# A gated DeltaNet layer reordered: decays from running sums, half of z's product between the quarters of q and k, later heads between output chunks

## The chip, the cores and the metric

The kernel runs on one core of a Trainium2 chip. The metric is the device time of one execution in microseconds (us), from the start of the program to its end. Work inside a core is shared by five engines, each with its own in-order queue: TensorE (PE in the profile; PEld is its weight load), VectorE (DVE), ScalarE (ACT), GpSimd (POOL) and SyncE (SP). Transfers between the chip's memory (DRAM) and the on-chip memory (SBUF) are issued from the SP, ACT and POOL queues and run on 16 DMA engines. Matmul results land in PSUM, which VectorE and ScalarE read.

## What is computed

The reference is a decoder trunk of two layers on 256 tokens with 2048 features, in float32. Layer 0 mixes tokens with an mLSTM, layer 1 with a gated DeltaNet; each layer then attends to 256 memory tokens and applies a squared-ReLU MLP with 8192 hidden features. Each sub-layer is wrapped in two RMS norms. The change concerns the DeltaNet, cut here to what matters (16 heads of q and k, 32 heads of v, 128 features each, chunks of 64 tokens):

```python
p = h @ w_in
qkv, z, bt, a = jnp.split(p, GDN_SPLITS, axis=-1)
qkv = jax.nn.silu(causal_dwconv(qkv, conv_w))
q = l2_norm(q) * (GD_K ** -0.5);  k = l2_norm(k)
beta = jax.nn.sigmoid(bt)
g = -jnp.exp(a_log) * jax.nn.softplus(a + dt_bias)
gam = jnp.cumsum(to_chunks(g), axis=-1)
diff = gam[..., :, None] - gam[..., None, :]
A   = einsum(kb, kc) * exp(where(strict, diff, -inf))     # unit triangular systems
U   = triangular_solve(A, vb);  W = triangular_solve(A, kb * exp(gam))
Aqk = einsum(qc, kc) * exp(where(causal, diff, -inf))
# recurrence over chunks gives o, then
o = rms_norm(o, norm_g) * jax.nn.silu(z)
return o @ w_out
```

The decay between two tokens is the exponential of a difference of running sums of g.

## The kernel before

**Products.** Every weight matrix is streamed once from DRAM in units of 1 MB (class `Weights`, lines 35 to 109). The order of units is a list written out at the start (`plan`, lines 127 to 153), and every product takes the next unit from it. A unit comes in two halves of 512 KB on SP's queue; each half is split into a high part (ScalarE, L88) and a low part (VectorE, L89), so that two or three fp32r matmuls stand for one of full precision. Two units are in flight. The splits are issued under `high_priority(offset=400)` (L100), which ranks them 400 instructions earlier than their place in the code; the Tile framework orders each engine's queue ahead of time by rank, among the instructions that it expects to be ready. Three forms of product exist: `prod_feat` (L316, L317) with features on partitions, `prod_tall` (L335 to L337), which makes one block of 128 features from a unit of 2048 x 128 weights with 48 matmuls of 256 columns, and `prod_tok` (L380 to L382) with tokens on partitions, 24 matmuls of 512 columns a unit and 96 for a chunk of 512 output columns.

**The DeltaNet layer**, `gdn` (from L860), has these stages:

1. *Quarters of q and k* (loop at L1017). Quarter c makes four heads of q (`prod_q`) and of k (`prod_k`), each feature block with its convolution (`conv`, L873: a product into a padded tile on VectorE, a scaling on ScalarE, three multiply-adds on VectorE at L883, SiLU on ScalarE). After the first k come the gates g and beta (`gates`, L916).
2. *Norms and pairs.* `norms(c)` takes the L2 norms of the quarter (squares at L975, sums by matmul at L979). `pairs(grp)` serves a group of four v heads (two k heads): `decays(grp)` makes the exponentials, two matmuls a k head (L996, L997) make the products of keys and queries, VectorE applies norms and causal masks (L999, L1001) and multiplies with the decays (L1007) into a tile `at`, of which there is one buffer; it is stored to DRAM on GpSimd's queue (L1009, L1014). In the kernel before, the norms and the first group of quarter c-1 come behind q of quarter c, and the second group behind k of quarter c; the last two groups come inside v's product.
3. *decays* (L937). GpSimd multiplies a triangular mask with g's high and low parts (L946, four products of 128 x 512 a group), TensorE sums them with six matmuls of 512 columns a group (L950) into PSUM slots named gep, and ScalarE takes twelve exponentials of 128 x 128 from them (L954).
4. *v and the solver* (L1080). Eight chunks of v, stored to DRAM token by token (`store_v`), with the triangular systems solved on VectorE between them (`solve`, L1042: the load of its inputs `work` and `rki` on GpSimd's queue at L1058 and L1046, a first product at L1061, then 31 steps).
5. *Heads and output* (L1218). For each half of the heads: four times a chunk of z (`prod_tok("gz")`, with SiLU on ScalarE into `zs`) followed by the group's `core` (L1099: loads, block inverses, products with v, norm, gate, transposes, split into y), then four chunks of the output product `g_out` over that half. The result of the first half is kept in SBUF and the second half is added.

**Buffers.** PSUM has three slots for short products (`psum`) and five for accumulators (`acc`). The pool `acts` has one buffer a tag: `h0` to `h15` hold the layer's input h, `u0` to `u15` and `y0` to `y3` are reused by stage.

## Time and profile before

| | us |
|---|---|
| median of three runs | 2935.88 |
| the three runs | 2935.88, 2927.8, 2936.1 |
| the profiled execution | 2926.02 |
| its span, first to last instruction | 2924.3 |

The profiler times one execution; a row of its views gives the engine, the line of the kernel, the operation, the tile written and the tiles read, the shapes, a count, and then busy time, mean duration in ns, and the idle time of that engine just before, with what ended it. Matmuls overlap one another, so what a matmul takes of PE's order is read from start to start in the timeline, not from its duration; a full f32 matmul leaves two records. By the timeline, the DeltaNet layer's own products begin at about 1244 us. The quarters of q and k run from there to about 1472, v's product from there to 1683, the heads and the output product from 1683 to about 2129. Layer 0 lies before, the second layer's attention and MLP behind.

### The profile page before, as it was taken

The numbers are of one execution on the slowest core, as the hardware profiler recorded it, in microseconds if no ns is written. First come the engines' busy times: TensorE is split into PE (matmuls) and PEld (weight loads), VectorE is DVE, ScalarE is ACT, GpSimd is POOL, SyncE is SP. The second block draws the span as 40 slices with busy tenths as digits, with TensorE's granted clock in tenths as the row PEclk, the third lists the DMA queues.
The fourth block names the chain that finished last, engine by engine and source line by source line (L and its number), as shares of the span: only waits on it lengthen the run. The fifth ranks groups of instructions, "written<-read, shape, count | busy, mean of one in ns | idle before, by whom it ended". The sixth has DMA issues, their size and how long they took to land.

```text
span 2924.3 us, 42593 instructions
## 1 busy us (share of the span) xinstructions
PE 2870.3 (98%) x16723; PEld 2479.6 (85%) x16723; DVE 1758.4 (60%) x2538; ACT 1458.4 (50%) x2221; POOL 159.7 (5%) x298
## 2 busy tenths in 40 slices
PE   8999999999999999999999999999999999999998
PEld 7888887888888888799999978888878888888887
DVE  5555656754645555588787955445576545455565
ACT  6444545644434444467775445445465444344443
POOL 0000000000000000003232131010000000000000
PEclk9999999999999999999999999999999999999999
DMA  7545564555555565666678775665545555555555
GB/s 243 186 146 172 192 202 130 187 190 193 187 189 188 192 195 185 208 157 192 187 211 231 219 263 197 207 196 180 199 142 176 192 189 187 192 187 193 192 187 166
DMA packets 375884, 557.65 MB, mean 191 GB/s; under 512 B 23409, under 2 KB 156274, under 8 KB 373378
## 3 DMA queue, kind: packets, MB, share of 16 engines
q1 hardware_dynamic: 363456, 507.12, 55.0%
q0 software_dynamic: 10656, 46.48, 4.6%
q8 instruction: 131, 2.15, 0.3%
q10 hardware_dynamic: 1570, 1.33, 0.1%
q14 instruction: 71, 0.58, 0.1%
HBM read 529.65 MB, written 25.20 MB: 190 GB/s over the span
## 4 chain that ended last, share of the span: by engine, by line
PE 44%; DVE 3%; DMA 2%; issue 1%; ACT 1%; POOL 0%; DVEq 0%; ACTq 0%; POOLq 0%
PE up L316 8%; PE down L380 4%; PE down L381 4%; PE down L382 4%; PE up L317 4%; PE g_out L381 2%; PE g_out L382 2%; PE g_out L380 2%; PE gz L380 2%; PE gz L382 2%; PE gz L381 2%; DVE lo L89 1%; PE op L1191 1%; DVE cv L883 1%; PE gv L336 1%
## 5 line engine op out<-in xcount | busy, mean ns | idle before, releaser
L89 DVE TENSOR_TENSOR lo<-raw,hi 128x1024 fp32r<-128x1024 f32 x938 | 1112.0, 1226 | 903.1 <-ACT hi L88 901.1
L88 ACT CAST hi<-raw 128x1024 fp32r<-128x1024 f32 x938 | 936.6, 1045 | 962.9 <-PE down L382 327.1
L316 PE MATMUL up<-h,hi 128*128 128x512 f32 x1920 | 678.7, 399 | 0.0
L317 PE MATMUL up<-h,lo 128*128 128x256 f32 x1920 | 539.9, 281 | 0.0
L316 PEld LDWEIGHTS up<-h,hi 128*128 128x128 f32 x1920 | 361.2, 188 | 89.2
L381 PE MATMUL down<-lo,u 128*128 128x512 f32 x1024 | 398.8, 390 | 0.0
L380 PE MATMUL down<-hi,u 128*128 128x512 f32 x1024 | 398.8, 389 | 0.0
L382 PE MATMUL down<-hi,u 128*128 128x512 f32 x1024 | 398.7, 389 | 0.0
L317 PEld LDWEIGHTS up<-h,lo 128*128 128x128 f32 x1920 | 363.3, 189 | 0.2
L382 PEld LDWEIGHTS down<-hi,u 128*128 128x128 f32 x1024 | 192.3, 188 | 40.1
L380 PEld LDWEIGHTS down<-hi,u 128*128 128x128 f32 x1024 | 192.3, 188 | 39.9
L381 PEld LDWEIGHTS down<-lo,u 128*128 128x128 f32 x1024 | 192.3, 188 | 39.5
L337 PE MATMUL gv<-h,lo 128*128 128x256 f32 x512 | 146.1, 285 | 4.8 <-DVE lo L89 4.8
L335 PE MATMUL gv<-h,hi 128*128 128x256 f32 x512 | 147.1, 287 | 0.0
L336 PE MATMUL gv<-h,hi 128*128 128x256 f32 x512 | 145.2, 284 | 0.0
L381 PE MATMUL gz<-lo,h 128*128 128x512 f32 x256 | 102.6, 401 | 1.8 <-DVE lo L89 1.8
L380 PE MATMUL gz<-hi,h 128*128 128x512 f32 x256 | 103.0, 402 | 0.1
L337 PEld LDWEIGHTS gv<-h,lo 128*128 128x128 f32 x512 | 98.2, 192 | 5.7 <-DVE lo L89 5.6
L382 PE MATMUL gz<-hi,h 128*128 128x512 f32 x256 | 102.4, 400 | 0.0
L381 PE MATMUL g_out<-lo,u 128*128 128x512 f32 x256 | 100.9, 394 | 0.5 <-DVE lo L89 0.5
L380 PE MATMUL g_out<-hi,u 128*128 128x512 f32 x256 | 100.6, 394 | 0.0
L382 PE MATMUL g_out<-hi,u 128*128 128x512 f32 x256 | 100.1, 393 | 0.0
(426 smaller groups left out, 4711.3 us busy)
## 6 DMA issues: line engine op xcount, KB each, us to landing
raw<-in_w_up SPq DMA_DIRECT2D x256, 512.0 KB, 3.9
raw<-in_w_down SPq DMA_DIRECT2D x256, 512.0 KB, 4.1
raw<-in_gdn_w_in SPq DMA_DIRECT2D x192, 512.0 KB, 4.9
raw<-in_mlstm_w_in SPq DMA_DIRECT2D x96, 512.0 KB, 4.2
raw<-in_gdn_w_out SPq DMA_DIRECT2D x64, 512.0 KB, 4.2
raw<-in_mlstm_w_out SPq DMA_DIRECT2D x32, 512.0 KB, 4.2
at_d<-at POOLq DMA_DIRECT2D x8, 1536.0 KB, 8.0
ab<-at_d POOLq DMA_DIRECT2D x8, 1536.0 KB, 6.9
```

What stands on the lines that cost most here:

```text
L88: a = nc.scalar.copy(h_, raw[:, :, :n])
L89: return a, nc.vector.tensor_tensor(l_, raw[:, :, :n], h_, ALU.subtract)
L316: PE.matmul(a[:fw], wh, srcs[kk][:, :], start=(kk == 0), stop=False, skip_group_check=True)
L317: PE.matmul(a[:fw, T:], wl, srcs[kk][:, 0:T], start=False, stop=(kk == nk - 1), skip_group_check=True)
L335: PE.matmul(a[:, 0:T], hi[k], srcs[k][:, 0:T], start=(k == 0), stop=False)
L336: PE.matmul(a[:, 0:T], hi[k], srcs[k][:, T:], start=False, stop=False)
L337: m = PE.matmul(a[:, 0:T], lo[k], srcs[k][:, 0:T], start=False, stop=(k == nk - 1))
L380: PE.matmul(accs[t], sh, hi[j], start=(kk == 0), stop=False)
L381: PE.matmul(accs[t], sh, lo[j], start=False, stop=False)
L382: PE.matmul(accs[t], sl, hi[j], start=False, stop=(kk == nk - 1))
L883: V.scalar_tensor_tensor(c, pad[:, j : j + T], w[j], c, ALU.mult, ALU.add)
L1191: PE.matmul(op[:, hh * P : (hh + 1) * P], aq[:, 1 if st else tt * 2, hh, :], w[:, st, hh * P : (hh + 1) * P], start=(hh == 0 and st == 0), ...
```

## The change

- **Decays.** The running sum of g within the 128 tokens of a tile is made once in `gates`, by two small matmuls with tokens on partitions (`cum`) and two with heads on partitions (`cumr`). `cumr` is stored to DRAM (`g_d`) and read back for each group as two tiles of 128 x 4 x 128 in which every partition holds the same rows (`load_rows`, on GpSimd's queue, two groups ahead). `decays` then forms the differences on VectorE, twelve `tensor_scalar` of 128 x 128 a group, and ScalarE takes two exponentials of 768 columns, in place. GpSimd's products, the matmuls of L950 and the split of g into two parts go.
- **Masks.** The two causal masks lie in one tile, and the eight masked products of a group become four of twice the width.
- **z.** The second half of z's product (chunks 4 to 7) moves between the quarters: quarter c makes q, k, the norms, the first group, one chunk of z (`early_z`: SiLU, store to DRAM `z_d`) and the second group. The weight plan follows. All groups are done when v's product begins.
- **Heads.** Groups 0 to 3 have their chunk of z before them as they had. Groups 4 to 7 are issued each before one of the first half's four output chunks (`later`, through the new argument `start` of `prod_tok`), with z read back from DRAM; their y is kept in the tiles of h, which is no longer needed.
- **Rank of the splits.** The offset of `high_priority` is a field `first`, 0 everywhere but in the DeltaNet layer, where it is 400 as before.

```diff
-                with self.tc.high_priority(offset=400):
+                with self.tc.high_priority(offset=self.first):
...
                 if c == 0:
                     ws.add("ab", g_in, 0, D, GDN_QKV + GDN_Z, 64, tall=True)
+                ws.add("gz", g_in, 0, D, GDN_QKV + 2048 + c * 512, 512)
             ws.add("gv", g_in, 0, D, 4096, 4096, tall=True)
+            ws.add("gz", g_in, 0, D, GDN_QKV, 2048)
             for half in range(2):
-                ws.add("gz", g_in, 0, D, GDN_QKV + half * 2048, 2048)
                 ws.add("g_out", g_out, half * 2048, 2048, 0, D)
...
+            masks = sc.tile([P, 2, P], F32, name="masks")
+            V.tensor_copy(masks[:, 0, :], tri_lt)
+            V.tensor_copy(masks[:, 1, :], tri_le)
...
                 PE.matmul(p_[:, 0:32], tri_gt, g[:, 0, :], start=True, stop=True)
+                for t in range(2):
+                    PE.matmul(p_[:, 32 + t * 32 : 64 + t * 32], tri_le, g[:, t, :], start=True, stop=True)
+                    PE.matmul(p_[0:32, P + t * P : 2 * P + t * P], g[:, t, :], tri_le, start=True, stop=True)
+                cumr = sc.tile([32, 2 * P], F32, name="cumr")
+                V.tensor_copy(cumr, p_[0:32, P : 3 * P])
+                nc.gpsimd.dma_start(g_d, cumr)
...
+            def load_rows(grp):
+                rows_of[grp] = []
+                for tt in range(2):
+                    r_ = acts.tile([P, 4, P], F32, tag=f"u{8 + grp % 2 * 2 + tt}", name="grow")
+                    src = g_d[grp * 4 : grp * 4 + 4, tt * P : (tt + 1) * P]
+                    nc.gpsimd.dma_start(r_, src.unsqueeze(0).to_broadcast([P, 4, P]))
+                    rows_of[grp].append(r_)
...
             def decays(grp):
                 dm = [acts.tile([P, 2, 3, P], F32, tag=f"y{grp % 2 * 2 + i}", name="gdm") for i in range(2)]
+                gr = rows_of.pop(grp)
+                for kh in range(2):
+                    for v2 in range(2):
+                        hh = kh * 2 + v2
                         hv = grp * 4 + hh
+                        for tt in range(2):
+                            V.tensor_scalar(dm[kh][:, v2, tt, :], gr[tt][:, hh, :], cum[:, tt, hv : hv + 1],
+                                            cml[:, tt, hv : hv + 1], ALU.min, ALU.subtract)
+                        V.tensor_scalar(dm[kh][:, v2, 2, :], gr[1][:, hh, :], sufb[:, hv : hv + 1], None, ALU.add)
+                    S.activation(dm[kh], dm[kh], AF.Exp)
+                if grp + 2 < GV_H // 4:
+                    load_rows(grp + 2)
                 return dm
...
+            def early_z(c):
+                def ev(ch, t, a):
+                    o_ = acts.tile([P, 512], F32, tag=f"u{14 + t}", name="zst")
+                    S.activation(o_, a, AF.Silu, scale=rs.tok[:, t : t + 1])
+                    nc.gpsimd.dma_start(z_d[c, :, t, :], o_)
+                prod_tok("gz", h, 1, ev)
...
             for c in range(4):
                 prod_q(c)
-                if c:
-                    norms(c - 1)
-                    pairs(c * 2 - 2)
                 prod_k(c)
                 if c == 0:
-                    lnb, gh, gl, sufb = gates()
-                else:
-                    pairs(c * 2 - 1)
+                    cum, cml, sufb = gates()
+                    load_rows(0)
+                    load_rows(1)
+                norms(c)
+                pairs(c * 2)
+                early_z(c)
+                pairs(c * 2 + 1)
             prod_v(0)
-            norms(3)
-            pairs(6)
             prod_v(1)
-            pairs(7)
             store_v(0)
...
+            y = new_u()
+            for g4 in range(4):
+                zs = gate(g4)
+                if g4 == 0:
+                    store_v(7)
+                core(g4, zs, y[g4 * 4 : g4 * 4 + 4])
+            y2 = new_h()
+
+            def later(ch):
+                zs = sc.tile([P, 2, 512], F32, tag="zs", bufs=2, name="zs")
+                nc.gpsimd.dma_start(zs, z_d[ch])
+                core(4 + ch, zs, y2[ch * 4 : ch * 4 + 4])
+
+            prod_tok("g_out", y, 4, lambda ch, t, a: post.add(ch, t, a, True), start=later)
+            prod_tok("g_out", y2, 4, lambda ch, t, a: post.take(ch, t, a, True), post=post)
...
         else:
+            ws.first = 400
             with tc.tile_pool(name="g0", bufs=1) as g0:
                 post = gdn(g0, h, xs)
+            ws.first = 0
```

More of the change, by code (lines that the diff above doesn't have):

```diff
@@ L354, in prod_few, with prod_tok @@
         return p_[:, 0 : 2 * n].rearrange("p (t n) -> p t n", t=2)
-    def prod_tok(key, srcs, n_ch, evac, after=None, post=None, stagger=False):
+    def prod_tok(key, srcs, n_ch, evac, after=None, post=None, stagger=False, start=None):
         nk = len(srcs)
         for c in range(n_ch):
+            if start:
+                start(c)
             accs = [acc(f"{key}{c}_{t}") for t in range(2)]
@@ L904, in gdn @@
         with tc.tile_pool(name="gd1", bufs=1) as sc:
-            tri_gt_r = sc.tile([P, P], F32R, name="tri_gt_r")
-            V.tensor_copy(tri_gt_r, tri_gt)
-            ones_r = sc.tile([P, P], F32R, name="ones_r")
-            V.tensor_copy(ones_r, ones)
+            masks = sc.tile([P, 2, P], F32, name="masks")
+            V.tensor_copy(masks[:, 0, :], tri_lt)
+            V.tensor_copy(masks[:, 1, :], tri_le)
             dtb = sc.tile([P, 32], F32, name="dtb")
@@ new lines, in gates @@
+                V.tensor_tensor(cml, cum, lnb, ALU.subtract)
+                return cum, cml, sufb
+            rows_of = {}
+            def load_rows(grp):
[5 more added lines that the diff above has]
+                    rows_of[grp].append(r_)
@@ L937, in decays @@
             def decays(grp):
                 dm = [acts.tile([P, 2, 3, P], F32, tag=f"y{grp % 2 * 2 + i}", name="gdm") for i in range(2)]
-                for blk, tt, lhs in ((0, 0, tri_gt_r), (1, 1, tri_gt_r), (2, 1, ones_r)):
-                    ep = psum("gep")
-                    if blk < 2:
-                        rr = []
-                        for i, src in enumerate((gh, gl)):
-                            r_ = acts.tile([P, 4, P], F32R, tag=f"u{8 + 2 * tt + i}", name=f"gl{tt}{i}")
-                            G.tensor_tensor(r_, tri_le[:, None, :].to_broadcast([P, 4, P]),
-                                            src[:, tt, grp * 4 : grp * 4 + 4].unsqueeze(2).to_broadcast([P, 4, P]), ALU.mult)
-                            rr.append(r_)
-                    for i in range(2):
-                        PE.matmul(ep, lhs, rr[i].rearrange("p h i -> p (h i)"), start=(i == 0), stop=(i == 1))
-                    for hh in range(4):
-                        hv = grp * 4 + hh
-                        b_ = sufb[:, hv : hv + 1] if blk == 2 else lnb[:, tt, hv : hv + 1]
-                        S.activation(dm[hh // 2][:, hh % 2, blk, :], ep[:, hh * P : (hh + 1) * P], AF.Exp, bias=b_)
@@ L1216, in core, with gate @@
                         split_into(ys[h2 * 2 + i], tp[:, i * T : (i + 1) * T], cols[:, COL_GDN : COL_GDN + 1])
-            for half in range(2):
-                y = new_u()
-                for g4 in range(4):
-                    zs = sc.tile([P, 2, 512], F32, tag="zs", bufs=2, name="zs")
-                    prod_tok("gz", h, 1, lambda ch, t, a: S.activation(zs[:, t, :], a, AF.Silu, scale=rs.tok[:, t : t + 1]))
-                    if half == 0 and g4 == 0:
-                        store_v(7)
-                    core(half * 4 + g4, zs, y[g4 * 4 : g4 * 4 + 4])
-                prod_tok("g_out", y, 4, (lambda ch, t, a: post.take(ch, t, a, True)) if half else
-                         (lambda ch, t, a: post.add(ch, t, a, True)), post=post if half else None)
+            def gate(g4):
+                zs = sc.tile([P, 2, 512], F32, tag="zs", bufs=2, name="zs")
+                prod_tok("gz", h, 1, lambda ch, t, a: S.activation(zs[:, t, :], a, AF.Silu, scale=rs.tok[:, t : t + 1]))
+                return zs
+            y = new_u()
[6 more added lines that the diff above has]
+            def later(ch):
+                zs = sc.tile([P, 2, 512], F32, tag="zs", bufs=2, name="zs")
+                nc.gpsimd.dma_start(zs, z_d[ch])
+                core(4 + ch, zs, y2[ch * 4 : ch * 4 + 4])
+            prod_tok("g_out", y, 4, lambda ch, t, a: post.add(ch, t, a, True), start=later)
+            prod_tok("g_out", y2, 4, lambda ch, t, a: post.take(ch, t, a, True), post=post)
         return post
```

20 lines of the change are left out of this document (10 added, 10 removed).

## The prediction

> **What bounds the kernel now.** The page comes first, then the chain, then PE's waits.
>
> ```profile
> span 2924.3 us, 42593 instructions
> PE 2870.3 (98%) x16723; PEld 2479.6 (85%) x16723; DVE 1758.4 (60%) x2538; ACT 1458.4 (50%) x2221; POOL 159.7 (5%) x298
> ```
>
> The reader is to see that TensorE (PE) is busy nearly all of the time, and no other engine is above 60% beside its weight loads. A matmul that PE needn't run shortens the kernel, as long as nothing else becomes late. 54 us are left in which PE is idle. The view of waits says who ends that idle time; I quote those that the change can touch and the largest that it leaves alone.
>
> ```profile
> PE ltp L212 <- DVE xk L492: 12.9, 8, 3.2
> PE gv L337 <- DVE lo L89: 4.8, 4, 2.5
> PE xo L380 <- ACT hi L88: 2.8, 2, 1.9
> PE g L997 <- ACT gdm L954: 2.2, 1, 2.2
> ```
>
> The first row belongs to the seams between sub-layers. The second and the fourth lie in the DeltaNet layer. The busy time by stage shows that layer: three quarters of q and k (the first three rows), then v's product while the triangular systems are solved.
>
> ```profile
> core 0: us, PE busy (x) PEld busy (x) DVE busy (x) ACT busy (x) POOL busy (x), PEclk, DMA share, GB/s
> 1322.00:1382.20 60.20, 57.73 (x442) 54.60 (x442) 48.73 (x77) 43.88 (x73) 20.03 (x31) 1.00 0.68 192
> 1382.20:1440.40 58.20, 57.95 (x446) 54.86 (x445) 47.28 (x75) 44.28 (x74) 19.42 (x34) 1.00 0.70 201
> 1440.40:1498.20 57.80, 57.80 (x447) 55.03 (x447) 46.53 (x76) 44.31 (x74) 20.29 (x34) 1.00 0.72 205
> ...
> 1557.00:1610.00 53.00, 49.19 (x407) 48.58 (x407) 39.74 (x68) 25.36 (x38) 10.34 (x23) 1.00 0.82 237
> 1610.00:1683.00 73.00, 72.02 (x602) 71.78 (x601) 68.85 (x117) 34.60 (x52) 9.13 (x20) 1.00 0.79 225
> ```
>
> In a quarter DVE is busy for 47.3 of 58.2 us (81%) and PE doesn't wait. In 1557 to 1610 PE loses 3.8 us. The clock column is 1.00 throughout, so no throttle enters the sum.
>
> **The change part by part. First, the decays.** Six matmuls a group (L950) go. I price them by what they take of PE's order, start to start, since a matmul's own duration overlaps the next.
>
> ```profile
> 1352.67 1.09 PE L950 MATMUL gep<-gl,tri_gt_r 128*128 128x512 f32 x4
> 1353.60 0.63 PE L950 MATMUL gep<-gl,ones_r 128*128 128x512 f32 x2
> 1354.07 0.28 PE L335 MATMUL gq<-h,hi 128*128 128x256 f32 x1
> ```
>
> From 1352.67 to 1354.07 are 1.40 us for the six of one group. Eight groups make 11.2 us, on the path, because PE has other work ready behind them. What comes instead on PE is four plain f32 matmuls in gates(), once: two of 32 columns and two of 128.
>
> ```profile
> 1314.80 0.30 PE L932 MATMUL suf<-g,tri_gt 128*128 128x32 f32 x2
> 1314.94 0.36 PE L337 MATMUL gq<-h,lo 128*128 128x256 f32 x1
> ```
>
> ```profile
> 1338.96 0.59 PE L997 MATMUL g<-gqk 128*128 128x256 f32 x2
> 1339.21 0.47 PE L337 MATMUL gk<-h,lo 128*128 128x256 f32 x1
> ```
>
> One of 32 columns takes 0.14 us (two records), one of 256 columns 0.25; so the four cost between 0.56 and 0.78, and I take 0.6. The net is 10.6 us off PE.
>
> The L950 products also held PSUM slots of the pool of three until ScalarE had taken the exponentials out. That is the 2.2 us row of g L997 <- gdm L954 above: the only such wait, and nothing of it remains when the exponentials read SBUF. I credit 2.2. What could be late next at this place is g's own slot, which DVE empties at L999 and L1001; it is so today in every other group without a wait of this size.
>
> The work that moves to other engines is this.
>
> ```profile
> L883 DVE SCALAR_TENSOR_TENSOR cv<-pad,cols,cv 128x256 f32<-128x256 f32 x100 | 54.4, 577 | 1.0 <-ACT gm L1003 0.2
> L999 DVE SCALAR_TENSOR_TENSOR gm<-g,rk,tri_lt 128x128 f32<-128x128 f32 x16 | 5.6, 348 | 9.0 <-PE g L996 9.0
> L954 ACT ACTIVATE gdm<-gep,lnb 128x128 f32<-128x128 f32 x64 | 18.6, 368 | 0.2
> L975 ACT ACTIVATE l2sq<-gqk 128x512 f32<-128x512 f32 x14 | 8.2, 644 | 0.0
> L88 ACT CAST hi<-raw 128x1024 fp32r<-128x1024 f32 x70 | 69.9, 1047 | 32.6 <-issue 15.3 <-PE gv L336 6.9 <-PE gq L336 3.7
> L89 DVE TENSOR_TENSOR lo<-raw,hi 128x1024 fp32r<-128x1024 f32 x69 | 88.5, 1323 | 9.7 <-ACT hi L88 9.7
> L946 POOL TENSOR_TENSOR gl<-tri_le,gl 128x512 fp32r<-128x512 f32 x16 | 21.6, 1352 | 0.0
> L946 POOL TENSOR_TENSOR gl<-tri_le,gh 128x512 fp32r<-128x512 f32 x16 | 18.0, 1122 | 33.9 <-PE gep L950 29.1 <-DVE sufb L934 4.8
> ```
>
> ```profile
> L883 DVE SCALAR_TENSOR_TENSOR cv<-pad,cols,cv x100: 393/480/4601, 1297.5 to 1545.7; 128x256 f32<-128x256 f32 x100
> ```
>
> ```profile
> L850 DVE TENSOR_SCALAR sp_r<-sp_u x1: 228/228/228, 1304.9 to 1304.9; 128x128 f32<-128x128 f32 x1
> ```
>
> ScalarE: twelve exponentials of 0.37 us a group (4.4) become two over 768 columns; between 0.64 (512 columns) and 1.05 (1024) I take 0.85 each, 1.7 in all. DVE: twelve tensor_scalar come in. The nearest row is L850 at 0.23 us, the upper bound is L999's 0.35, which reads PSUM: 2.8 to 4.2 us a group, and I take 2.8. The eight mask products of 0.35 become four of twice the width, priced by L883's median of 0.48: 2.8 becomes 1.9. GpSimd: the four products a group go. With them goes what they did to DVE: L883 has a median of 480 ns but a mean of 577 and one instruction of 4601 ns, and 97 ns times 100 are 9.7 us of DVE time over the stage, 2.4 a quarter.
>
> The Trainium skill (SBUF — State Buffer, "Who interferes with whom") states that a DVE instruction with two SBUF inputs and a GpSimd instruction that reads SBUF exclude each other for the length of the one that came first. By that rule up to all 39.6 us of the two L946 rows come off DVE, 9.9 a quarter, where L883's rows show 2.4. The trace agrees in kind (the 4601 ns). The page speaks against the change as well, under "SBUF: two separate sides": one-input DVE work in its faster mode, which tensor_scalar can be, locks out the descriptor writing of GpSimd's DMAs, and that would delay the new row loads; no run here shows it. The sum stays the same by both; they move the first rival's chance only, in opposite directions.
>
> **Second, z between the quarters.** Sixteen weight units move forward, with every DMA and split that they issue, on SP's queue in the same order as the plan. Their matmuls cost the same anywhere.
>
> ```profile
> 1909.82 0.39 PE L382 MATMUL g_out<-hi,u 128*128 128x512 f32 x1
> 1910.05 0.39 PE L380 MATMUL gz<-hi,h 128*128 128x512 f32 x1
> ```
>
> The first row is the end of one chunk and the second the start of the next, 0.23 us apart. A chunk of 96 is 22 us of PE. A quarter then has 58.2 - 2.8 + 22 = 77.4 us of PE. DVE gets 47.3 + 8 x 1.32 (z's subtractions) + 2 x (2.8 - 0.9) - 2.4 = 59.3 us, 77%, and 80% with the dearer tensor_scalar; it was 81%. ScalarE gets 44.3 + 8 x 1.05 + 2 x 0.64 - 2 x 2.7 = 48.6, 63%; it was 76%. So the extra product is paced by PE. It is also the cover that the new order needs: the squares for norms(c) now follow k's convolution at once, where q's product of the next quarter stood between (23 us); the z chunk of 22 us takes that place. Were this cover gone, one chain would stand on PE: four DVE operations near L883's 0.48 and three ScalarE operations up to 0.64, about 4 us a quarter and 16 in all. That needs PE's order to put the norms ahead of a product that is ready; with half of it I bound the new order's waits at +8, and at -2 below, and take +1.
>
> The new DMAs on GpSimd's queue (two row loads a group, two z stores a quarter) queue ahead of the stores of A and the three-column memsets that each convolution needs. Rows are asked for two groups ahead, a whole quarter of 77 us (groups 0 and 1 only when the gates are done, but no matmul waits for their decays); accumulators are five deep and a tall unit uses one, so a late memset has four units to catch up. I price both at nothing; if this cover fails, the price is the one of the next paragraph.
>
> **Third, the solver.** In the kernel before, groups 6 and 7 are still at work inside v's product, so the solver's inputs are queued late on GpSimd, and DVE runs into them:
>
> ```profile
> 1581.65 2.29 DVE L1061 TENSOR_TENSOR solve_w<-solve_w,rki 128x2048 f32<-128x2048 f32 x1 [2.28 <-DMA rki<-rk_d]
> ```
>
> ```profile
> 1584.25 2.35 DVE L89 TENSOR_TENSOR lo<-raw,hi 128x1024 fp32r<-128x1024 f32 x2
> ```
>
> ```profile
> 1585.53 0.38 PE L337 MATMUL gv<-h,lo 128*128 128x256 f32 x1 [2.47 <-DVE lo L89]
> ```
>
> DVE waits 2.28 us for the load and takes 2.29 for the product; the weights' low halves queue behind both, and PE loses 2.47. After the change all pairs end about when v's product starts, so the load lands before DVE gets there, and the twelve steps behind it don't pile up. Of the 4.8 us in the wait row I credit 3.3, between 0 and 4.8.
>
> **Fourth, later heads' cores.** Cores 4 to 7 run beside the first half's four output chunks, 4 x 22 = 88 us of PE, instead of beside z. The same matmuls interleave, and z's SiLU is read back from DRAM. I take 0, between -2 and +2.
>
> **Fifth, splits outside this layer** lose their rank of 400 instructions. That reorders ScalarE and DVE everywhere; the trace shows no such order. In the MLP there is room for it:
>
> ```profile
> 707.64 2.36 DVE L89 TENSOR_TENSOR lo<-raw,hi 128x1024 fp32r<-128x1024 f32 x2 [3.08 <-ACT hi L88]
> ```
>
> ```profile
> L401 DVE TENSOR_TENSOR j_up<-up,h_up 128x256 f32<-128x256 f32 x21 | 8.4, 419 | 0.0
> ```
>
> A unit's two subtractions take 2.36 us after 3.08 us idle. A feature's three DVE operations (0.42 each) are 1.3, which fit. Softmax chains at the seams would go ahead of splits. I take -1, between -9 (half of the 12.9 + 2.8 + 2.2 us of waits at such chains) and +63 (rival 2).
>
> The sum: -10.6 - 2.2 - 3.3 + 1 + 0 - 1 = -16.1 us. The profiled execution took 2926.0 (span 2924.3 and 1.7 around it), which gives 2910. The median of the three runs, 2935.9, lies 9.9 above it, so I forecast 2935.9 - 16 = 2920.
>
> **The rivals.** (1) The quarters are held by DVE's order, not by PE. Both groups of a quarter now crowd around the z chunk; if an instruction there waits for a late row load, or an `at` product for the stores of the group before, the low halves queue behind it as at L1061, and the 11.2 us come back as PE waits for lo. That gives 2931, no difference to be told. Against it: 77% DVE, and no such wait in 1440 to 1498. (2) The splits without rank come late in the MLP. If all four features of a chunk (4 x 1.26 = 5.0 us) go ahead of the two subtractions, 3.08 us of idle time cannot hold them, PE waits 2.0 us a chunk, and 2 layers x 16 chunks cost 63: 2983, slower. It decides once more than 3.08 us go ahead, that is three features; against it, three of the four are complete before the unit ends. (3) The seams gain their 9 us: 2911. For it, the ScalarE casts that precede softmax work; against it, much of the seams' order is fixed by hand.
>
> **How the numbers follow.** Forecast 0.65, rival one 0.14, rival two 0.09, rival three 0.12. A measurement can tell about 0.3% (8.8 us) from no change, so faster means below 2927. Forecast and rival three make 0.77 faster, less 0.02 for the forecast's upper tail: 0.75; same 0.16; slower 0.09. The range goes from 2898 (2911 less what the solver and the new order may give beyond my values, 1.5 + 3, and the 8.1 by which the fastest run lies under the median) to 2940 (2920 with +7 from the new order, +3.3 without the solver's gain, +2 for the cores and the same 8). It leaves out rival two.
>
> **What would show it.** Right: no L950; three quarters of about 77 us each with PE idle under 1 us; L883's mean near 480 ns; the wait of L1061 for rki gone, and 1557 to 1610's counterpart without its 3.8 us; PE's busy total about 11 us lower. Wrong: new PE waits for lo inside the quarters, a DVE wait for the row loads, or PE waits for hi or lo in the up products.

## The result, and the profile after

The changed kernel takes 2911.37 us (median of four executions, 2910.57 to 2916.84). The kernel before, timed beside it, takes 2932.49 (four, the three of the table above among them, 2927.8 to 2936.1). The ratio is 0.9929, with a 95% interval of 0.9916 to 0.9943: 21 us less, faster by more than twice what a measurement can tell. The forecast was 2920 with a range of 2898 to 2940. So the sign and the range held and the middle was 9 us high. As the experiments show, though, the sum came near for partly other reasons than the prediction gave.

The profiled execution after took 2910.57 us, that of before 2926.02, so the traces differ by 15.5 us. That of before is a fast one, 6.5 us under its median, and the traces show 5.6 us less than the medians do. The page of the changed kernel, its size and TensorE's row:

```profile
span 2908.8 us, 42441 instructions
PE 2866.5 (99%) x16683; PEld 2478.6 (85%) x16683; DVE 1756.9 (60%) x2603; ACT 1427.3 (49%) x2127; POOL 142.3 (5%) x295
```

PE runs 40 records fewer: 48 of L950 went and 8 small ones came. It is busy only 3.8 us less, though the records that went alone were 11.5 us of its order, by their starts in the timeline. Something made other matmuls longer. Next, those of PE's waits in the changed kernel that the text below needs, in total, times and longest:

```profile
PE ltp L214 <- DVE xk L496: 10.9, 9, 1.8
PE gv L337 <- ACT hi L89: 3.2, 1, 3.2
PE np L1156 <- DMA ab<-at_d: 2.3, 1, 2.3
PE gv L339 <- DVE lo L90: 1.7, 2, 0.9
PE g L1018 <- ACT gm L1023: 1.6, 1, 1.6
```

The waits of gv for lo (4.8 before) and of g for gdm (2.2 before) have shrunk or gone. The second, third and fifth row are new, and each ends on a step of the new order or the new decays. The busy time by stage follows: three quarters and the start of v's product (columns as in the prediction: PE, PEld, DVE, ACT, POOL, clock, DMA share, GB/s).

```profile
1325.20:1402.70 77.50, 77.50 (x531) 70.86 (x530) 64.64 (x123) 58.63 (x74) 18.02 (x38) 1.00 0.79 235
1402.70:1480.40 77.70, 77.70 (x533) 71.11 (x531) 58.92 (x103) 50.54 (x65) 16.75 (x37) 1.00 0.81 243
1480.40:1556.50 76.10, 76.10 (x529) 70.29 (x527) 54.55 (x86) 45.31 (x60) 12.80 (x30) 1.00 0.76 216
1556.50:1610.00 53.50, 51.14 (x417) 50.08 (x416) 36.39 (x52) 23.08 (x34) 11.00 (x21) 1.00 0.94 247
```

These are the quarters that the prediction drew: about 77 us each, PE never idle, DVE at 72 to 83%. VectorE's multiply-adds no longer meet GpSimd's products; in the rows of their line the median stands at 479 ns and the longest at 491, where the longest of before was 4601:

```profile
L889 DVE SCALAR_TENSOR_TENSOR cv<-pad,cols,cv x192: 465/479/491, 1267.5 to 1761.9; 128x256 f32<-128x256 f32 x192
```

What made matmuls longer in this trace is TensorE's clock. Cut at the steps of the clock's record, two places of the changed kernel read like this:

```profile
1307.88:1311.30 3.42, 3.42 (x26) 2.94 (x27) 0.68 (x4) 2.28 (x3) 0.52 (x1) 1.00 0.61 161
1311.30:1314.71 3.41, 3.41 (x13) 3.04 (x14) 0.65 (x4) 0.53 (x2) 3.02 (x4) 0.50 0.38 74
1314.71:1318.12 3.41, 3.41 (x10) 2.64 (x9) 1.01 (x3) 1.56 (x2) 0.00 (x0) 0.50 0.79 233
1318.12:1321.54 3.42, 3.42 (x15) 2.49 (x14) 3.42 (x9) 2.23 (x4) 0.00 (x0) 1.00 0.38 94
...
1744.80:1748.21 3.41, 0.33 (x2) 0.30 (x2) 1.30 (x2) 2.37 (x3) 0.00 (x0) 1.00 1.05 425
1748.21:1751.62 3.41, 2.50 (x12) 2.29 (x11) 2.77 (x5) 0.90 (x3) 0.00 (x0) 0.50 1.00 401
1751.62:1755.04 3.42, 3.42 (x18) 3.42 (x17) 1.96 (x2) 1.93 (x3) 0.00 (x0) 0.50 0.80 270
```

In the rows with a clock of 0.50 PE seems as busy as ever, but a matmul of 512 columns takes 0.43 us from start to start (gz from 1314.58 on) where the prediction's rows had 0.23. The second block shows what came before: in the step from 1744.80 PE had work for 0.33 us of 3.41. In the first block PE seems busy in the step before, largely with the norm's sums (l), which are two columns wide; sixteen records of them, which are eight sums, take 1.81 us:

```profile
1307.59 1.95 PE L1000 MATMUL l<-ones,l2sq 128*128 128x2 f32 x16
1309.40 1.10 PE L1017 MATMUL g<-gqk 128*128 128x512 f32 x2
```

In the two spans half clock lasts 15.3 us before and 37.6 us after, so at most 7.7 and 18.8 us of work are lost to it. But these are single executions, and that of the kernel before is one of its best, with a mean granted clock of 0.997. Over the 55 executions of the kernel before in the four groups below, that clock is 0.994 in the mean (0.992 to 0.997, about 18 us lost); in the changed kernel's four it is 0.994, 0.992, 0.991 and 0.995 (about 20 us). So half clock explains where this trace loses time. As a difference between the two kernels it is worth only some 3 us.

Where the 15.5 us of the profiled executions lie, by the first and last product of the DeltaNet layer: its first product starts at 1235.9 where it started at 1243.9 (-8.0), the layer takes 880.1 us where it took 885.2 (-5.1), and what follows takes about 2.4 less. The prediction had it the other way round: -15 in the layer and -1 outside it. Here too the fast execution of the kernel before counts: its layer holds 2.8 us of half clock and the changed kernel's 20.5, so the two traces show too little gain in the layer.

Two theories stand against each other from here. **A**: the rank of the splits is worth some 10 us, the decays their 13, and the new order costs about 5, through stalls that halve the clock behind them. **P**: the terms of the prediction are right (rank -1, decays -12.8, the order with the solver's gain -2), and the rest is scatter between two executions.

### The profile page after: what moved, and what is told of

It reads as the page before. It is cut to its first block, busy times and chain, and to the rows that moved or that the text cites. A ratio compares the mean times of both kernels' runs of the same rounds, so it can differ in the third digit from the quotient of the medians.

```text
span 2908.8 us, 42441 instructions
## 1 busy us (share of the span) xinstructions
PE 2866.5 (99%) x16683; PEld 2478.6 (85%) x16683; DVE 1756.9 (60%) x2603; ACT 1427.3 (49%) x2127; POOL 142.3 (5%) x295
## 4 chain that ended last, share of the span: by engine, by line
PE 90%; DVE 4%; DMA 3%; ACT 1%; issue 1%; POOL 0%; DVEq 0%; ACTq 0%; POOLq 0%
PE up L318 15%; PE up L319 8%; PE down L384 8%; PE down L385 8%; PE down L386 8%; PE o L318 2%; PE g_out L386 2%; PE g_out L384 2%; PE g_out L385 2%; DMA raw<-in_gdn_w_in 2%; PE gz L384 2%; PE gz L386 2%; PE gz L385 2%; DVE lo L90 1%; PE gk L337 1%
## 5 line engine op out<-in xcount | busy, mean ns | idle before, releaser
L337 PEld LDWEIGHTS gv<-h,hi 128*128 128x128 f32 x512 | 99.2, 194 | 3.8 <-ACT hi L89 3.4
L338 PEld LDWEIGHTS gv<-h,hi 128*128 128x128 f32 x512 | 99.2, 194 | 0.2 <-issue 0.2
L889 DVE SCALAR_TENSOR_TENSOR cv<-pad,cols,cv 128x256 f32<-128x256 f32 x192 | 90.9, 480 | 6.3 <-ACT cv L887 3.8
```

The costliest lines, as they stand in the source:

```text
L337: PE.matmul(a[:, 0:T], hi[k], srcs[k][:, 0:T], start=(k == 0), stop=False)
L338: PE.matmul(a[:, 0:T], hi[k], srcs[k][:, T:], start=False, stop=False)
L889: V.scalar_tensor_tensor(c, pad[:, j : j + T], w[j], c, ALU.mult, ALU.add)
```

## The experiments

Each kernel ran interleaved with the kernel before on the same chip. In the four groups the latter's medians were 2933.3, 2931.9, 2934.1 and 2930.7, so ratios are compared, and absolute times only roughly.

### The rank alone, and everything but the rank

The kernel before with the rank taken off outside the DeltaNet layer:

```diff
-                with self.tc.high_priority(offset=400):
+                with self.tc.high_priority(offset=self.first):
```

> The kernel before with one edit: outside the DeltaNet layer the splits lose their rank of 400. Theory A (from the two traces: the first product of the DeltaNet layer starts at 1235.9 us after the change and at 1243.9 before it, and the products behind the layer take 2.4 us less): the rank alone is worth about 10 us, so 2922, a ratio of 0.9965. Rival P (the prediction's own term of -1 us, the difference between the traces being scatter of two executions): 2931, a ratio of 0.9997. Under A the waits of PE for low and high halves outside the layer (xo, and ltp for xk) shrink; under P they stay.

Measured: 2919.29, ratio 0.9957 [0.9942, 0.9971], 12.6 us less. The other way round, the changed kernel with the old rank:

```diff
-                with self.tc.high_priority(offset=self.first):
+                with self.tc.high_priority(offset=400):
```

> The changed kernel with the rank of 400 put back everywhere. Theory A: it loses the rank's 10 us of the 21 that the change brought, so 2921 to 2922, a ratio to the kernel before of 0.9963, and its DeltaNet layer begins near 1244 us again. Rival P: it loses 1 us, 2912, a ratio of 0.9931.

Measured: 2917.81, ratio 0.995 [0.9937, 0.9963]. Against the changed kernel's 0.9929 the rank brings 0.0021 there, 6 us, and 12.6 alone. P's -1 falls; A holds, with a size between 6 and 12.6. For the 6, the intervals of the two ratios just overlap. In both pairs of traces the layer's first product starts 8 to 9.5 us earlier without the rank (1243.9 and 1235.9; 1245.4 and 1235.9).

The place can be read. These are the two largest waits of PE around the first cross attention (440 to 530 us; total, times, longest) in the kernel before:

```profile
PE ltp L212 <- DVE xk L492: 5.4, 3, 3.2
PE xo L380 <- ACT u L245: 1.6, 1, 1.6
```

and the largest in the kernel without the rank:

```profile
PE ltp L213 <- DVE xk L493: 3.5, 3, 1.8
```

ScalarE in the kernel before, in order of time, at the seam behind that attention:

```profile
518.64 1.05 ACT L88 CAST hi<-raw 128x1024 fp32r<-128x1024 f32 x1 [1.51 <-DMA raw<-in_w_up]
519.59 0.59 ACT L230 ACTIVATE junk<-xo 128x512 f32<-128x512 f32 x1
```

ScalarE stands 1.51 us in front of a split whose weights have not landed, because the rank put the split first. Behind it waits the sum of squares (junk) that closes the norm, and behind that norm waits all of PE: the seam's longest wait is 3.2 us, and half clock follows at 523.1. Without the rank the longest is 1.8 and the clock stays whole there (it halves once at 454.6, ahead of this seam, where the kernel before kept it). All of PE's waits from 440 to 530 us sum to 9.4 us before and to 5.3 without the rank, and the first product of the MLP behind the seam starts at 518.5 instead of 525.5 us: most of the 8 us by which the DeltaNet layer starts earlier are won up to here. An urgent instruction in an in-order queue holds back all that is behind it, if its own input is late.

### The decays alone

The kernel before with the new decays and wide masks, in the old order:

```diff
-                    lnb, gh, gl, sufb = gates()
+                    cum, cml, sufb = gates()
+                    load_rows(0)
+                    load_rows(1)
...
-                        S.activation(dm[hh // 2][:, hh % 2, blk, :], ep[:, hh * P : (hh + 1) * P], AF.Exp, bias=b_)
+                            V.tensor_scalar(dm[kh][:, v2, tt, :], gr[tt][:, hh, :], cum[:, tt, hv : hv + 1],
+                                            cml[:, tt, hv : hv + 1], ALU.min, ALU.subtract)
...
+                    S.activation(dm[kh], dm[kh], AF.Exp)
```

> The kernel before with the new decays and the wide masks alone, in the old order and with the old rank. Both theories: the matmuls of gep go (-11.2), four small ones come (+0.6), the PSUM wait of g for gdm goes (-2.2): 2920, a ratio of 0.9956. Rival D (VectorE held the quarters in part, so the twelve new tensor_scalar a group give some of it back): 2927 or more, a ratio of 0.998 or above, with new waits of PE for lo inside the quarters.

Measured: 2927.39 (twelve executions, 2922.2 to 2936.17), ratio 0.9982 [0.997, 0.9994]: 5.3 us less where both theories said 13. Rival D gave that time, but by another mechanism: it expected waits for lo inside the quarters. The profiled execution took 2936.2, the upper end of the twelve, so its trace shows the cost at its largest. PE's largest wait outside the seams is this:

```profile
PE gv L335 <- ACT hi L88: 10.1, 3, 6.3
```

It lies in v's product. ScalarE's wait there for the weights (1472 to 1700 us), in the kernel before:

```profile
ACT hi L88 <- DMA raw<-in_gdn_w_in: 14.4, 8, 4.0
```

and with the new decays in the old order:

```profile
ACT hi L88 <- DMA raw<-in_gdn_w_in: 22.9, 5, 10.4
```

The weights come up to 10.4 us late where it was 4.0. The stretches of this kernel around the two stalls show what else is under way, and what follows:

```profile
1565.00:1576.00 11.00, 10.40 (x86) 10.40 (x87) 5.83 (x8) 5.01 (x8) 5.47 (x10) 1.00 1.08 287
1576.00:1583.00 7.00, 1.93 (x12) 1.43 (x10) 5.67 (x7) 2.42 (x3) 0.00 (x0) 0.73 0.74 211
1583.00:1590.00 7.00, 6.71 (x33) 6.71 (x34) 6.93 (x17) 3.13 (x5) 0.20 (x2) 0.54 0.67 172
...
1665.00:1681.00 16.00, 16.00 (x136) 16.00 (x135) 8.54 (x14) 5.08 (x9) 5.07 (x6) 1.00 1.04 288
1681.00:1688.00 7.00, 0.75 (x7) 0.54 (x5) 1.08 (x1) 2.16 (x3) 0.00 (x0) 0.79 0.93 379
```

Ahead of each stall the DMA share is over 1.0: the solver's inputs and zeros at the first, its results (3 MB) at the second, all on the same 16 DMA engines as the weights. PE idles 5.1 and 6.3 us, and then runs at half clock. The matmuls of L950 are gone and most of the time that they took is not: PE got ahead of the transfers and waits for them. The clock adds to it. This trace has 34.1 us of half clock in the layer, 13.7 of them in the quarters, behind steps that hold the norm's sums; over the twelve executions the mean clock is 0.992, against 0.994 for the kernel before beside them, which is up to 4 of the 8 us that are missing.

### The order alone

The kernel before with z between the quarters and the later heads between the output chunks, with the old decays, masks and rank:

```diff
-                if c:
-                    norms(c - 1)
-                    pairs(c * 2 - 2)
                 prod_k(c)
...
+                norms(c)
+                pairs(c * 2)
+                early_z(c)
+                pairs(c * 2 + 1)
...
+            prod_tok("g_out", y, 4, lambda ch, t, a: post.add(ch, t, a, True), start=later)
```

> The kernel before with the new order alone (z between the quarters, later heads between the output chunks), with the old decays, masks and rank. Theory A: the order by itself costs; in the changed kernel's trace the 384 matmuls of z between the quarters take 92.3 us where 87.4 were due, and new waits stand in front of gv (3.2 us) and np (2.3 us) with half-clock stretches behind them, against a solver wait saved of 3.3: 2934 to 2940, a ratio of 1.0005 to 1.003. Rival P (the prediction's terms: solver -3.3, order +1, cores 0): 2930, a ratio of 0.9992.

Measured: 2936.84 (twelve executions), ratio 1.0014 [1.0005, 1.0022], 4 us slower: theory A. Its waits:

```profile
PE gv L337 <- ACT hi L89: 6.6, 1, 6.6
PE gq L339 <- DVE lo L90: 2.9, 3, 1.3
PE np L1141 <- DMA ab<-at_d: 2.0, 1, 2.0
```

The first is the solver's results again, which now meet PE at the end of v's product; the second shows quarters that hold both the old decays and z's chunk, and is absent in the changed kernel; the third is the later heads.

Decays alone -5, order alone +4, both together (the kernel without the new rank) -15: some 13 us are in the combination, well clear of the intervals.

### What the combination does: the groups out of v's product

The decays alone as above, and the groups of a quarter directly behind its own k, without z:

```diff
-                if c:
-                    norms(c - 1)
-                    pairs(c * 2 - 2)
                 prod_k(c)
...
                     load_rows(1)
-                else:
-                    pairs(c * 2 - 1)
+                norms(c)
+                pairs(c * 2)
+                pairs(c * 2 + 1)
             prod_v(0)
-            norms(3)
-            pairs(6)
             prod_v(1)
-            pairs(7)
```

> The kernel with the new decays in the old order, and one more edit: norms and both groups of a quarter come directly behind the quarter's own k, with no chunk of z between them, so that the last two groups leave v's product; the rank and the heads are as before. Theory V (alone the decays gained 5 us where 13 were due because their last two groups meet the solver's loads and stores inside v's product, where the weights came up to 10 us late): 2920, a ratio of 0.995 to 0.996, and v's stage near 200 us. Rival C (the chunk of z is the cover that the groups need: ScalarE's exponentials wait for VectorE's differences and hold the casts of the weights up, in every quarter): 2927 to 2937, a ratio of 0.998 to 1.001, with PE waits for hi or lo in gq and gk, about 4 us a quarter.

Measured: 2920.97, ratio 0.9964 [0.9951, 0.9976], 10.5 us less. Theory V gave the time, rival C falls: no chunk of z is needed to cover the groups, and PE's longest wait for hi or lo in gq and gk is under 1 us. But V's own sign failed. v's stage takes 212.6 us in the profile, not 200 (221.6 with the decays alone, 200.8 in the changed kernel), and the transfers still hold the weights up, by PE's waits and by ScalarE's for the raw weights in v's product (23.8 us, the longest 10.8):

```profile
PE gv L335 <- ACT hi L88: 11.4, 2, 6.6
```

So 5 of the 13 us come back when the groups stand behind their own quarter and the last two leave v's product (the intervals of the two kernels, 0.997 to 0.9994 and 0.9951 to 0.9976, just overlap). By these traces, weights that come less late are not how: both waits are as long as with the decays alone. How the 5 us come back is not shown. The rest comes with z's chunk and the later heads; that it does so by giving the transfers more time is argued and not shown.

### The half clock: its trigger

By the clock's record of all 14 profiled kernels, a change of clock starts only on a grid of 3.413 us (in the changed kernel 1311.30 lies 22 steps behind 1236.21, and 1748.21 another 128). Each full-speed step from 300 us on was sorted by how long PE had matmuls in it. All 68 steps filled for less than 0.43 were followed by half clock. Between 0.43 and 0.59 both occur. Above 0.59, eleven of more than 10,000 were, and each of these holds the norm's sums (l, two columns wide). Such sums alone are not enough: some 190 steps hold them, and twelve of these (the eleven, and one filled for less than 0.43) were followed by half clock. What else is in the step separates them. Without the matmuls of 32 columns and fewer, counted from start to start, the twelve steps are filled for 0.44 at most and all the others for 0.50 or more.

The same stall costs differently by its place on the grid. In the changed kernel the wait of np falls into one step:

```profile
1959.84:1963.25 3.41, 1.07 (x34) 1.02 (x35) 3.10 (x4) 1.79 (x3) 0.00 (x0) 1.00 0.85 332
1963.25:1966.66 3.41, 3.41 (x10) 2.64 (x9) 0.50 (x2) 0.00 (x0) 0.00 (x0) 0.50 0.78 281
```

In the kernel before, the solver's wait of 2.47 us was cut in two by the grid, and nothing followed:

```profile
1581.20:1584.61 3.41, 1.85 (x17) 1.65 (x15) 2.96 (x3) 0.51 (x2) 0.10 (x1) 1.00 0.42 102
1584.61:1588.02 3.41, 2.49 (x20) 2.50 (x21) 3.41 (x7) 0.69 (x2) 0.00 (x0) 1.00 0.33 80
```

The Trainium skill (TensorE: Matmul & The Clock Gate, "HAM oscillation — how this bites in real kernels") asks for no idle gaps of PE over about 3.4 us. The runs here are stricter: 2.3 us in one step were enough, and so was none at all where the matmuls were two columns wide.

A test of the second kind puts the first quarter's norms ahead of the gates, so that their sums lie among other matmuls:

```diff
                 if c == 0:
+                    norms(0)
                     cum, cml, sufb = gates()
                     load_rows(0)
                     load_rows(1)
-                norms(c)
+                else:
+                    norms(c)
```

> The changed kernel with the first quarter's norms issued ahead of the gates, so that their sums (128 x 2 matmuls, l) lie between other matmuls and not in a block with the running sums. Theory G (the half clock from 1311.3 to 1318.1 us in the changed kernel answers to a 3.41 us stretch filled with matmuls of a few columns): the granted clock near 1311 stays 1.00 or halves for 3.41 us less, and the time falls by 1.7 to 3.4 us, so about 2908.5, a ratio to the kernel before of 0.9918. Rival N (the half clock there has another cause, or a stall moves in): the clock halves there as it did and the ratio stays 0.9929.

Measured: 2908.09, ratio 0.9916 [0.9901, 0.993], 3 us less than the change by itself; the intervals overlap. The half clock at 1311 is gone, as theory G has it, and the mean clock of its five executions is 0.995, against 0.993 for the changed kernel's four. One step of it comes at 1335.8 instead, behind a stall that the edit itself makes, a product of keys and queries that waits for its PSUM slot:

```profile
PE g L1018 <- DVE gm L1021: 3.4, 1, 3.4
```

### The stalls of the new order, one by one

**The solver's results as whole rows.** Four stores of 4 KB a partition with the zeros in them, in place of rows of 32 and two stores of zeros:

```diff
...
-                    V.tensor_copy(tn[i], td[i].rearrange("p c i -> p i c"))
-                    r_ = slice(i * 32, i * 32 + 32)
-                    nc.gpsimd.dma_start(tn_d[:, r_, r_], tn[i])
+                    V.tensor_copy(tn[i][:, :, i // 2 * 32 : i // 2 * 32 + 32], s_.rearrange("p c i -> p i c"))
+                    nc.gpsimd.dma_start(tn_d[:, i * 16 : i * 16 + 16, :], tn[i])
```

> The changed kernel with the solver's transposed blocks stored as whole rows of 64 with their zeros (four tiles of 128 x 16 x 64, 4 KB of a partition contiguous) in place of rows of 32 and two stores of zeros. Theory S (the weights at the end of v's product arrive late, 14.6 to 15.7 us after their issue, because the solver's stores of 128-byte rows hold the DMA engines at a share of 1.0): PE's 3.2 us wait of gv for hi shrinks below 1.5 us and its half clock of 6.83 us goes: -4 to -6 us, 2906, a ratio of 0.991. Rival B (it is the bytes, 2 MB of t_d and 1.5 MB of the first ab load, not the small rows): the wait stays at 2 to 3.5 us and the ratio at 0.9929.

Measured: 2913.47, ratio 0.9936 [0.9921, 0.9951]. Theory S falls for these stores, which are 1 of the 3 MB; the wait grows:

```profile
PE gv L337 <- ACT hi L89: 5.5, 1, 5.5
```

The weights' landing in that stretch shows little change, in the changed kernel (KB each, median us from issue to landing):

```profile
raw<-in_gdn_w_in SPq DMA_DIRECT2D x4, 512.0 KB, 14.6
```

and with whole rows:

```profile
raw<-in_gdn_w_in SPq DMA_DIRECT2D x4, 512.0 KB, 13.6
```

**The first load of ab later**, behind the last store of v:

```diff
+                if grp == 0:
+                    behind(d_, stored[0])
```

> The changed kernel with the first core's load of ab (1.5 MB, issued at 1732.8 us into the solver's stores) put behind the last store of v. Rival B of the run before (the bytes decide): 1.5 of about 5 MB leave the burst, at the 266 to 410 GB/s of that stretch some 4 to 5 us of DMA time, so the 3.2 us wait of gv and its half clock go: -4 to -6 us, 2906, a ratio of 0.991. Theory S: the weights concerned were issued before that load matters, the wait shrinks by 1 us or less, ratio 0.9925 to 0.9929. A new wait of np or vp for ab at 1780 would show that it is now late.

Measured: 2912.53, ratio 0.9936 [0.9923, 0.9949], no gain. The wait of gv stays at 2.6, and a new wait has come at the first heads, at 1792.3 us, as the expectation warned. Its row names no transfer, but ab's load was issued only at 1781.9:

```profile
PE np L1158 <- issue: 3.3, 1, 3.3
PE gv L337 <- ACT hi L89: 2.6, 1, 2.6
```

**The solver's results in six pieces**, from ScalarE's queue, one behind each convolution of the last chunk of v:

```diff
-                nc.gpsimd.dma_start(t_d, tm)
...
+                for i in range(4):
+                    r_ = slice(i * 16, i * 16 + 16)
+                    behind(nc.scalar.dma_start(t_d[:, r_, :], tm[:, r_, :]), here[0])
+                    yield
...
```

> The changed kernel with the solver's results stored in six pieces (four of 512 KB of t_d, two of tn) from ScalarE's queue, one behind each convolution of the last chunk of v, in place of three stores at once. Theory B (the 3 MB at once hold the weights up: the first ab load's place and the width of the rows have been found not to matter): the pieces leave room for the weights between them, PE's wait of gv for hi at the end of v's product (2.5 to 3.3 us in four kernels, with 6.83 us of half clock behind it) falls below 1 us and the clock stays 1.00 there: -3 - 3.4 = -6 us, a ratio of 0.991 to the kernel before. Rival (the DMA engines are short for the whole stretch, whatever the order): the wait stays at 2 us or more, or is split into several, ratio 0.9929.

Measured: 2912.34, ratio 0.9929 [0.9915, 0.9942], no gain, and yet what theory B forecast for that stretch is seen. The weights of that stretch land in a median of 8.5 us instead of 14.6, PE is busy through it, and the clock stays whole:

```profile
1745.00:1752.00 7.00, 6.32 (x53) 6.12 (x53) 4.06 (x6) 3.38 (x5) 0.00 (x0) 1.00 1.00 366
...
1778.00:1781.40 3.40, 0.95 (x9) 0.71 (x7) 2.21 (x2) 3.29 (x5) 2.73 (x5) 1.00 0.63 222
1781.40:1784.80 3.40, 3.02 (x37) 2.60 (x38) 1.00 (x3) 0.25 (x1) 3.40 (x7) 0.50 0.94 289
```

The second and third of these stretches give it back, at the first heads 30 us later. GpSimd's queue tells why: the loads of tn stand behind the last piece, which landed only then.

```profile
1778.66 1.78 POOL L1148 DMA_DIRECT2D tn<-tn_d  x3 [11.64 <-DMA tn_d<-tn]
```

The stall at the end of v's product had been a matter of when 3 MB go out, and the next user of the same data was the next to be late. Pieces with tn first were not tried.

**ab in halves**, the one that np reads first:

```diff
-                nc.gpsimd.dma_start(ab, at_d[grp])
+                nc.gpsimd.dma_start(ab[:, 0:3], at_d[grp, :, 0:3])
+                nc.gpsimd.dma_start(ab[:, 3:6], at_d[grp, :, 3:6])
```

> The changed kernel with each load of ab in two halves, the one that np reads first. Theory L (the later cores follow each other every 26 us where it was 33 us, and the 1.5 MB of ab that wait for the buffer come 2.3 us too late): the wait of np for ab goes, and with it the half clock of 3.41 us at 1963: -2.3 - 1.7 = -4 us, 2907, a ratio of 0.9915. Rival (the two halves share the DMA engines, so the first lands hardly earlier): the wait stays above 1.5 us and the ratio at 0.9929.

Measured: 2905.21 (2901.24 to 2907.91), ratio 0.9908 [0.9894, 0.9922], 6 us less than the change by itself, where theory L forecast 4; the intervals just overlap. Theory L's signs have come: the half clock at 1963 is gone, and of the wait remains

```profile
PE np L1157 <- DMA ab<-at_d: 0.7, 1, 0.7
```

### Together

The first, pieces and halves in one kernel:

```diff
+                    norms(0)
...
+                nc.gpsimd.dma_start(ab[:, 0:3], at_d[grp, :, 0:3])
+                nc.gpsimd.dma_start(ab[:, 3:6], at_d[grp, :, 3:6])
...
+                    behind(nc.scalar.dma_start(t_d[:, r_, :], tm[:, r_, :]), here[0])
```

> The changed kernel with three edits: the first quarter's norms ahead of the gates, ab in halves, the solver's results in pieces. If the three gains are independent (-3.5 and -6 us measured for the first two, -6 forecast for the third), 2911 - 15.5 = 2896, a ratio of 0.988; if the pieces bring nothing, 2902, a ratio of 0.9898; if a stall that goes here comes back at the next late transfer, 2906 or more, 0.991.

Measured: 2908.5 (2903.52 to 2916.74), ratio 0.9915 [0.9901, 0.9929]: the third of the three expectations, a stall that comes back elsewhere (np waits 2.9, 2.0 and 1.8 us again). Without the pieces, norms and halves only:

```diff
+                    norms(0)
...
+                nc.gpsimd.dma_start(ab[:, 0:3], at_d[grp, :, 0:3])
+                nc.gpsimd.dma_start(ab[:, 3:6], at_d[grp, :, 3:6])
```

> The changed kernel with the two edits that gained by themselves, the first quarter's norms ahead of the gates (0.9916) and ab in halves (0.9908), and without the pieces of the solver's stores. If the gains add up: 0.9929 - 0.0013 - 0.0021 = 0.9895, 2902 us. If part of either was scatter, or a stall moves to where the other edit had freed the way: 0.991, 2907.

Measured: 2905.56 (2904.46 to 2907.94), ratio 0.9915 [0.9902, 0.9929]. The gains do not add up: on top of the norms the halves bring nothing in the ratio (0.9915 against 0.9916), though the half clock at 1963 is gone here too. So what ab in halves is worth lies between 0 and 6 us. Alone, at 2905.21, it is the fastest median that was found, about 27 us under the kernel before by its ratio (0.0092 of 2932); as the best of several that these intervals do not tell apart, it may be in part chance.

## Why the prediction held, point by point

**What bounds the kernel**: right. PE is busy 99% of the time, the quarters are paced by it, and the L950 matmuls were on the path.

**The decays**: 11.2 us were priced for L950, and 11.5 are gone from PE's order. The four small matmuls were priced at 0.6 and take 1.3 (from 1306.26 to 1307.59 in the timeline), since each costs 0.32 to 0.34, of 32 columns or of 128. The 2.2 us for gdm went, and the candidate that was named as late next, g's own slot, came with 1.6. VectorE and GpSimd went as drawn (a median of 479 ns). But "on the path, because PE has other work ready behind them" failed for the decays alone, which bring 5.3 us. Behind the removed matmuls the weights' transfers were late next, in v's product, and the prediction had not looked for them there.

**The solver**: the wait of gv for lo fell by 3.1 (3.3 credited). A wait for hi of 3.2 came in its place, behind the solver's results at the other end of v's product. The prediction watched the solver's loads and not its stores.

**The order**, at +1, and **later heads' cores**, at 0: the order alone costs 4 us, with new stalls of gv (6.6 there) and np (2.0). Its mean clock, 0.994, is that of the kernel before, so by this measure half clock is no part of that cost. On top of the new decays, though, the same order gains 9 us (0.9982 to 0.995). That the two need each other, 13 us in all, is the term that the prediction lacks; it added them up as if each stood alone. For the cores the price of 0 rested on "the same matmuls interleave"; what was missed is that in the changed kernel they follow each other after 25.7 to 28.4 us, the last after 33.8, where it was 30.3 to 33.2, with a load of 1.5 MB for one buffer between them. In the trace that is a wait of 2.3 us and a step of half clock.

**"No throttle enters the sum"** had no ground. The clock stood at 1.00 in the stretches that the prediction shows, but the kernel before runs at 0.994 in the mean of 55 executions, and a wait that goes or comes can take half clock with it or bring it. In the two traces the layer has 2.8 us at half clock before and 20.5 after, up to 9 us of work; over all executions the two kernels differ by only some 3.

**The rank**, at -1, was the largest miss of a single term: -6 to -12.6. Rival three had the mechanism (ScalarE's casts ahead of the chains at the seams) and, with 2911, the time; it got a chance of 0.12. The evidence against it, that much of the seams' order is fixed by hand, was no row of the trace. Of the 17.9 us of waits from which its 9 us are taken, 2.2 is, among the rows shown, the wait of g for gdm, which lies in the layer where the rank stays and is credited to the decays already. Rival two, the price of the same edit in the MLP, is refuted: the time between the first product up and the DeltaNet layer is 718.4 us before and 717.4 after.

So by the ratios everything but the rank brings 14.7 us, and the prediction's terms for it add up to 15.1. That this agrees is luck: alone, the decays fall 7.5 us short of their term, the order and the solver's gain miss theirs by 6, and a combination that was not priced makes up for both. The 5 us by which the whole change beat the sum of 16 are the rank's. Of the signs that were listed, four came as written (no L950, quarters of 77 us, 480 ns, no wait of the solver's first product for rki), and none of the signs of being wrong did. The counterpart of 1557 to 1610 still idles 2.4 us (51.14 of 53.5 busy), 1.6 of them at g's slot, and "PE's busy total about 11 us lower" was 3.8, since matmuls at half clock count as busy.

What stays open: why decays and order need each other, and with it why z's chunk between the groups brings the remaining 4 us over the groups without it; and whether the rank's 12.6 alone really becomes 6 in the changed kernel, or the intervals, which allow the same value for both, are all that is behind it.

## What to carry to other kernels

When a matmul that is not needed goes from a path that PE sets, look for the transfer that PE will now catch up with, bursts of stores most of all, before crediting the time. Changes that are priced one by one can need each other; the kernel with one of them alone shows it. A stall of 2 us can cost another 1.7 to 3.4 of work through the clock, so read the clock in windows of a few us, not by stage. But compare the clocks of many executions before saying that one kernel loses more by it than another: here the one trace of the kernel before was as good as the best of 55. A rank that pulls instructions forward in an in-order queue pays only if their inputs are there; look at what the queue holds behind them.

## What the hardware showed that was not expected

In these 14 traces TensorE's clock changed only on a grid of 3.413 us, and the filling of the step before decided: under 0.43 of a step with matmuls always halved it, over 0.59 never, except where matmuls of a few columns (eight sums of two columns in 1.81 us) made up most of the step. Repeated executions of one kernel spread by 14 us (2925.3 to 2939.5 over 23 of the kernel before in one group), and the clock goes with it: of the 55 executions in the four groups, the nine with a mean clock of 0.992 have a median of 2936.6 us, and the eight with 0.996 or more one of 2927.2. That the place of the stalls on this grid does it fits the two traces above, and was not tested.

Weights of 512 KB land in a median of 5.0 us over the changed kernel's DeltaNet layer, in 14.6 when 3 MB of stores are issued ahead of them, in 13.6 when 1 of these 3 MB goes out in rows of 4 KB and not of 128 bytes, and in 8.5 when the 3 MB go out in pieces.
